# Block products, seven for eight, in the FFN and mixer output projections, with the residual kept tokens x features

## The chip, the cores and the metric

The kernel runs on one core of one Trainium2 chip, in one launch. Its metric is the device time in microseconds of that core, from the start to the end of an execution. The core's engines each run their own instructions in a fixed order and meet through semaphores: TensorE (PE) multiplies matrices, and its weight loads run beside its matmuls; VectorE (DVE), ScalarE (ACT) and GpSimd (POOL) work elementwise; SyncE (SP) issues DMAs, and ACT and POOL can issue them too.

## The reference

A trunk of two layers over 512 tokens of 1024 features in fp32. Each layer is a half-step FFN, a mixer (HGRN2 in layer 0, forgetting attention, called fox, in layer 1) and a second half-step FFN; each of the six sub-layers takes the RMS norm of the residual and adds its result to it. The FFN is the SwiGLU with 2816 hidden features, so its input product is 512 x 1024 by 1024 x 5632, its output product 512 x 2816 by 2816 x 1024.

```python
def rmsnorm(x, g):
    return x * lax.rsqrt(jnp.mean(x * x, axis=-1, keepdims=True) + EPS) * g

def swiglu(h, w_in, w_out):
    gate, up = jnp.split(h @ w_in, 2, axis=-1)
    return (jax.nn.silu(gate) * up) @ w_out

for layer in range(2):
    x = x + 0.5 * swiglu(rmsnorm(x, norm_g[layer, 0]), ffn_w_in[layer, 0], ffn_w_out[layer, 0])
    hn = rmsnorm(x, norm_g[layer, 1])
    x = x + (hgrn2_mixer(hn, ...) if layer == 0 else fox_mixer(hn, ...))   # both end in o @ w_out, 1024 x 1024
    x = x + 0.5 * swiglu(rmsnorm(x, norm_g[layer, 2]), ffn_w_in[layer, 1], ffn_w_out[layer, 1])
```

## The kernel before

*Precision.* Every fp32 operand of the large products is split into two parts of a type that PE takes in one pass: ACT copies it to `h`, rounded, and DVE subtracts `h` from the operand to get `l` (`split_w`, L109: ACT at L113, DVE at L114). A product is then three matmuls into one PSUM bank, `h h`, `h l` and `l h` (`mm3`, L117). Weights come from DRAM in each layer and are split after the load.

*The residual* lies in `xT`, features x tokens: eight tiles of 128 features by 512 tokens. It is made at the start by 32 transposes of x and turned back by 32 at the end (`store`, L629), two tiles of features after each quarter of the last output product. When a tile of `xT` is updated, `norm_tile` (L130) at once makes the next layer's `xh` and `xl` from it, scaled by the norm's gain, and adds its squares up. The root itself is only known when all tiles are done; so the products run on the unnormed rows, and the factor of each token is multiplied onto their results: as a column where tokens are partitions (`norm_col`, L150, its root a power on POOL, L148), as a row spread over the partitions by four transposes where they are columns (`norm_bc`, L169).

*The FFN's input* (`ffn`, L245): 22 tiles of 128 hidden features. For each, the gate and the up product take 8 x 3 matmuls (eight tiles of input features, three parts) with weights of 128x128 and 512 tokens as moving columns (`proj_T`, L179). DVE multiplies both results by the norm's row (L269, L270), ACT does the Silu (L271), DVE the product with `us` (L272), and both split the result. Weights come in loads of 1 MB on SP's queue, two tiles of hidden features at a time.

*The output products* (`out_proj`, L213): four pairs of tiles of 128 output features. Each has 22 (FFN) or 8 (mixer) tiles of input features x 2 x 3 matmuls, again with 512 tokens moving.

*Order.* Pools have numbered buffers: two raw weight tiles, four `wh` and four `wl`, and PSUM banks by tag (three `mm`, two `lv`, two `ms`, one `po`). The order of instructions is that of a scheduler, which follows the program and takes what is ready; on the chip each engine keeps it. The mixers are long chains of their own; of them the change keeps the arithmetic between their input products and their output product.

In the names of tiles below, `f01` is layer 0's second FFN, `g` and `u` gate and up, `o` its output product, `ho` and `xo` the mixers' output products.

## Time and profile before

| What | us |
|---|---|
| median of 3 runs (2080.69 to 2081.03) | 2080.72 |
| the profiled execution | 2079.27 |
| its span, first to last instruction | 2077.5 |
| f00: input product, then output product, end at | 252.3, 372.0 |
| HGRN2, then its output product, end at | 619.2, 672.9 |
| f01: input, output, end at | 913.7, 1033.3 |
| f10: input, output, end at | 1274.1, 1393.8 |
| fox, then its output product, end at | 1642.9, 1708.5 |
| f11: input, output, end at | 1949.3, 2077.5 |

PE is busy in 99% of the span, DVE in 48%, ACT in 35%, POOL in 4%. A stage ends where the first matmul of the next one starts in the timeline of PE (the last one with the span). A busy share says how much of the time some instruction of an engine ran, and since matmuls run over one another, a duration of one is longer than the distance to the next one's start.

### The profile page before, as it was taken

The numbers are of one execution on the slowest core, as the hardware profiler recorded it, in microseconds if no ns is written. First come the engines' busy times: TensorE is split into PE (matmuls) and PEld (weight loads), VectorE is DVE, ScalarE is ACT, GpSimd is POOL, SyncE is SP. The second block draws the span as 40 slices with busy tenths as digits, with TensorE's granted clock in tenths as the row PEclk, the third lists the DMA queues.
The fourth block names the chain that finished last, engine by engine and source line by source line (L and its number), as shares of the span: only waits on it lengthen the run. The fifth ranks groups of instructions, "written<-read, shape, count | busy, mean of one in ns | idle before, by whom it ended". The sixth has DMA issues, their size and how long they took to land.

```text
span 2077.5 us, 23852 instructions
## 1 busy us (share of the span) xinstructions
PE 2059.2 (99%) x9853; PEld 1694.4 (82%) x9853; DVE 1007.1 (48%) x1473; ACT 727.9 (35%) x1083; POOL 77.9 (4%) x90
## 2 busy tenths in 40 slices
PE   8999999999999999999999999999999999999999
PEld 7888888888888888888888888888777778888887
DVE  6444423467566444433344443335566664444332
ACT  5232322333234332322232322227566643232211
POOL 0000000000000000000000000002122100000000
PEclk9999999999999999999999999999999999999999
DMA  5332322221212323322322322333222222232231
GB/s 167 101 102 85 113 92 96 85 76 56 75 60 82 102 81 103 101 97 92 107 91 86 117 82 96 110 98 97 82 68 74 88 72 91 86 117 81 97 116 52
DMA packets 193068, 190.70 MB, mean 92 GB/s; under 512 B 6144, under 2 KB 188848, under 8 KB 192960
## 3 DMA queue, kind: packets, MB, share of 16 engines
q1 hardware_dynamic: 192608, 188.93, 28.1%
q8 instruction: 77, 1.26, 0.2%
q14 instruction: 31, 0.25, 0.0%
q10 hardware_dynamic: 352, 0.25, 0.0%
HBM read 187.04 MB, written 2.13 MB: 91 GB/s over the span
## 4 chain that ended last, share of the span: by engine, by line
PE 94%; ACT 3%; DVE 1%; issue 0%; DMA 0%; SPq 0%
PE f11oy L118 2%; PE f11oy L119 2%; PE f10oy L120 2%; PE f10oy L118 2%; PE f01oy L120 2%; PE f01oy L119 2%; PE f00oy L119 2%; PE f00oy L118 2%; PE f11oy L120 2%; PE f10oy L119 2%; PE f01oy L118 2%; PE f00oy L120 2%; PE lv L358 2%; PE xo L561 1%; PE pT L553 1%; PE xvp L120 1%
## 5 line engine op out<-in xcount | busy, mean ns | idle before, releaser
L538 POOL TENSOR_TENSOR cbc<-cbc,cmask 128x128 f32<-128x128 f32 x64 | 35.3, 552 | 159.7 <-DVE mn L540 106.2
L358 PEld LDWEIGHTS lv<-Q,K 128*128 128x128 f32 x320 | 37.4, 192 | 3.7 <-issue 3.4
L358 PE MATMUL lv<-Q,K 128*128 128x64 f32 x320 | 38.8, 274 | 0.0
L543 ACT ACTIVATE PP<-PP,mn 128x512 f32<-128x512 f32 (+3 forms) x64 | 35.5, 556 | 4.1 <-DVE mn L540 3.4
L120 PE MATMUL xvp<-xvh,xl 128*128 128x256 f32 (+1 forms) x128 | 36.4, 285 | 0.0
L118 PE MATMUL xvp<-xvh,xh 128*128 128x256 f32 (+1 forms) x128 | 36.4, 284 | 0.0
L119 PE MATMUL xvp<-xvl,xh 128*128 128x256 f32 (+1 forms) x128 | 36.4, 284 | 0.0
L134 ACT ACTIVATE xh<-xT,gains 128x512 fp32r<-128x512 f32 x40 | 28.5, 712 | 14.4 <-DVE xT L238 14.4
L558 DVE COPY PP<-pT 128x512 f32<-128x512 f32 (+3 forms) x32 | 15.7, 492 | 35.9 <-PE pT L553 35.9
L553 PEld LDWEIGHTS pT<-ident,PP 128*128 128x128 f32 x160 | 17.0, 140 | 19.6 <-issue 13.2
L540 DVE CUSTOM_DVE_ANT_0 PP<-cbc,sc 128x512 f32<-128x512 f32 (+3 forms) x64 | 30.2, 480 | 3.3 <-PE xo L561 2.6
L135 DVE SCALAR_TENSOR_TENSOR xl<-xT,gains,xh 128x512 fp32r<-128x512 f32 x40 | 29.5, 747 | 4.0 <-ACT xh L134 4.0
L561 PE MATMUL xo<-PP,xV 128*64 128x512 f32 (+3 forms) x128 | 28.2, 458 | 0.0
L536 PE MATMUL sc<-KS,QH 128*128 128x512 f32 (+3 forms) x64 | 22.4, 350 | 5.1 <-DVE mn L540 3.8
L553 PE MATMUL pT<-ident,PP 128*128 128x128 f32 x160 | 24.5, 284 | 2.1 <-DVE PP L545 2.1
L545 DVE TENSOR_SCALAR PP<-PP,mn 128x512 f32<-128x512 f32 (+3 forms) x64 | 26.0, 408 | 1.0
L556 ACT COPY PP<-pT 128x512 f32<-128x512 f32 (+3 forms) x32 | 13.6, 426 | 35.3 <-PE pT L553 34.5
L119 PEld LDWEIGHTS xvp<-xvl,xh 128*128 128x128 f32 x128 | 24.4, 191 | 0.2
L118 PEld LDWEIGHTS xvp<-xvh,xh 128*128 128x128 f32 x128 | 24.4, 191 | 0.2
L120 PEld LDWEIGHTS xvp<-xvh,xl 128*128 128x128 f32 x128 | 24.4, 191 | 0.0
L142 DVE TENSOR_TENSOR acc<-acc,sq 128x512 f32<-128x512 f32 x35 | 24.0, 686 | 0.0
L536 PEld LDWEIGHTS sc<-KS,QH 128*128 128x128 f32 x64 | 12.0, 187 | 14.1 <-DVE mn L540 10.0
(2471 smaller groups left out, 6530.3 us busy)
## 6 DMA issues: line engine op xcount, KB each, us to landing
f01wg<-in_ffn_w_in_dram SPq DMA_DIRECT2D x11, 1024.0 KB, 4.9
f01wu<-in_ffn_w_in_dram SPq DMA_DIRECT2D x11, 1024.0 KB, 4.9
f10wg<-in_ffn_w_in_dram SPq DMA_DIRECT2D x11, 1024.0 KB, 5.1
f10wu<-in_ffn_w_in_dram SPq DMA_DIRECT2D x11, 1024.0 KB, 4.9
f11wg<-in_ffn_w_in_dram SPq DMA_DIRECT2D x11, 1024.0 KB, 5.0
f11wu<-in_ffn_w_in_dram SPq DMA_DIRECT2D x11, 1024.0 KB, 5.0
f00wg<-in_ffn_w_in_dram SPq DMA_DIRECT2D x10, 1024.0 KB, 4.9
f00wu<-in_ffn_w_in_dram SPq DMA_DIRECT2D x10, 1024.0 KB, 4.9
```

The costliest lines, as they stand in the source:

```text
L118: MM(out, lhsT=lh, rhs=rh, start=first, stop=False)
L119: MM(out, lhsT=lh, rhs=rl, start=False, stop=False)
L120: MM(out, lhsT=ll, rhs=rh, start=False, stop=last)
L134: nc.scalar.activation(st["xh"][:, k, :], xT[:, k, :], AF.Copy, scale=g)
L135: nc.vector.scalar_tensor_tensor(st["xl"][:, k, :], xT[:, k, :], g, r32(st["xh"][:, k, :]), op0=ALU.mult, op1=ALU.subtract)
L358: MM(pl[:, c], lhsT=Kc[:, c, :], rhs=Qv[:, c, :, 1, :], start=True, stop=True)
L536: MM(sc[:, :W], lhsT=QH[:, par, ts_], rhs=KS[:, par, :W], start=True, stop=False)
L538: nc.gpsimd.tensor_add(cb[:, ts_], cb[:, ts_], cmask)
L540: nc.vector.tensor_tensor_reduce(row, cb[:, :W].rearrange("p (b s) -> p b s", s=P), sc[:, :W].rearrange("p (b s) -> p b s", s=P), 1.0, 3.0e38,
L543: nc.scalar.activation(row, row, AF.Exp, scale=-1.0, bias=mn[:, t:t + 1], accum_out=sms[par][:, t:t + 1])
L553: nc.tensor.transpose(pT[:, (t - s) * P:(t - s + 1) * P], PPs[par][:, s, t, :], ident)
L561: MM(po[rows, s * P:], lhsT=V[:, s, (pr * 2 + par) * FD:(pr * 2 + par + 1) * FD], rhs=PPs[par][:, s, s:, :].rearrange("p t q -> p (t q)"), ...
```

## The change

*Seven products for eight.* Both matrices of a product are cut into 2 x 2 blocks. Instead of eight block products, sums of blocks are formed on both sides first, and seven products `p1` to `p7` are taken of them; their results are combined by additions. On the activations' side the operands are B11, B21, B22 and the sums T1 to T4; on the weights' side W11, W12, W22 and four sums. The weight sums are made in SBUF by DMAs of POOL's queue that add the loaded block to the tile (`accum_op`): one tile `x` holds W21, then W21+W22, then further blocks, and is split anew each time; one further sum, `s3`, is an addition on POOL. The activation sums are formed on DVE in the FFN's input and on POOL in its output.

*FFN input* (`steps_in`): the two halves of the tokens are the columns of the blocks, so a matmul moves 256 columns. There are 11 items of 256 hidden features from each half (the last with 128 of gate and 128 of up); each has 7 products of 2 x 4 x 3 matmuls, on blocks of 512 input features. ACT and DVE combine the results; the Silu stands on ACT.

*FFN and mixer outputs* (`steps_out`): the result is tokens x features, with weights as the moving operand, 512 columns, and activations as what PE holds. There are 7 products, each over 11 (or 4) tiles of input features x 2 tiles of tokens x 3.

*Residual and norm.* The residual `X` stays tokens x features from the load to the store. After an output product ACT squares it with the sums per token, POOL takes the root, ACT scales the rows by it, PE transposes them (`turn`), and the gain is multiplied on with the copy out of PSUM. The products' inputs are then normed already, so the multiplications by the norm's column or row go.

*Order.* One list of steps, a product or a part of one each, runs through consecutive layers (`Line`): work for a step is written a fixed number of steps ahead (loads 7 to 9, block sums 4 to 8, splits 3). Each tile has a numbered slot of one pool: five `wx` for `x` and `s3`, four `wr`, four `wh` and `wl`, and the eight PSUM banks in turn. The first two items of an FFN run p1, p1, p2, p2 ahead of the rest.

```diff
-    def out_proj(src, nkt, hl, scale, nxt, nm, tail=None, mid=None):
...
-                        if early and kks.start == 2:
-                            mid()
-                        for half in range(2):
-                            hs = slice(half * P, (half + 1) * P)
-                            for kk in kks:
-                                k = k0 + s0 + kk
-                                ah, al = hl[k]
-                                mm3(py[half], h[:, kk, hs], l[:, kk, hs], ah, al, k == 0, k == nkt - 1)
...
+    BUFS = {"ar": 4, "ar3": 2, "wx": 5, "wxs": 1, "wr": 4, "wh": 4, "wl": 4, "bh": 7, "bl": 7,
+            "p1": 3, "V2": 2, "V3": 2, "y": 2, "s": 8}
+    BYTES = {"ar": 8192, "ar3": 6144, "wxs": 2048, "p1": 2048, "V2": 2048, "V3": 2048, "y": 2048, "s": 128}
...
+        def scaled(self, j):
+            self.ys = []
+            for kh in range(2):
+                for t in range(2):
+                    y = at(("V2", "V3")[kh], [T], f"{self.id}y{j}{kh}{t}")
+                    c = 2 * j + t
+                    nc.scalar.activation(y, X[:, c, kh * T:(kh + 1) * T], AF.Copy, scale=rstd[:, c:c + 1])
+                    self.ys.append(y)
...
+            for kp in range(2):
+                pt = psum(f"{self.id}t{j}{kh}{kp}", (2, H))
+                for kk in range(2):
+                    for t in range(2):
+                        k = kp * 2 + kk
+                        nc.tensor.transpose(pt[:, kk, t * P:(t + 1) * P], self.ys[kh * 2 + t][:, k * P:(k + 1) * P], ident)
+                k = kh * 4 + kp * 2
+                if self.blocks:
+                    nc.vector.tensor_mul(self.gx[kh][:, j, kp * 2:kp * 2 + 2, :], pt,
+                                         self.g[:, k:k + 2].unsqueeze(2).to_broadcast([P, 2, H]))
+                    continue
...
+            b11, b12, b21, b22 = self.gx[0][:, 0], self.gx[0][:, 1], self.gx[1][:, 0], self.gx[1][:, 1]
+            nc.vector.tensor_sub(b11, b11, b12)
+            self.block("T1", b11)
+            nc.vector.tensor_sub(b12, b22, b12)
+            self.block("T3", b12)
+            nc.vector.tensor_add(b11, b11, b22)
+            self.block("T2", b11)
+            nc.vector.tensor_sub(b21, b21, b11)
+            self.block("T4", b21)
+            self.block("B22", b22)
...
+            def begin():
+                it["r11"] = load("wr", 0, 0, "r11")
+                it["x"] = load("wx", 0, 1, "x")
+            def sums():
+                it["s3"] = at("wx", [4, 256], n_ + "s3")
+                nc.gpsimd.tensor_add(it["s3"], it["r11"], it["x"])
+                acc(it["x"], 1, 1)
...
+            RAW = {"p1": "r11", "p5": "x", "p2": "r12", "p7": "s3", "p6": "x", "p4": "r22", "p3": "x"}
+            def split_of(p):
+                def what():
+                    it["split"][p] = split(it[RAW[p]], W_HL, [4, 256], f"{n_}{p}")
+                    if p == "p5":
+                        acc(it["x"], 0, 0)
+                    if p == "p6":
+                        acc(it["x"], 1, 0)
+                return what
...
+                    b = {"p2": "p1", "p3": "p5"}.get(p)
+                    if b is None:
+                        it["bank"][p] = psum(f"{n_}{p}", (2, H))
+                    bank = it["bank"][b or p]
+                    h, l = it["split"].pop(p)
+                    bh, bl = norm.B[OPERAND[p]]
+                    for s in range(2):
+                        ss = slice(s * P, (s + 1) * P)
+                        for k in range(4):
+                            mm3(bank[:, s, :], h[:, k, ss], l[:, k, ss], bh[:, k, :], bl[:, k, :],
+                                b is None and s == 0 and k == 0, s == 1 and k == 3, b is not None)
+                return what
...
+                def p6():
+                    it["V2"] = V2 = at("V2", [2, H], n_ + "V2")
+                    it["V3"] = V3 = at("V3", [2, H], n_ + "V3")
+                    nc.vector.tensor_sub(V2, it["p1s"], bank["p6"])
+                    nc.vector.tensor_add(V3, bank["p7"], V2)
+                    result(1, 1, lambda out: nc.vector.scalar_tensor_tensor(out, bank["p5"], -1.0, V3[:, :out.shape[1], :],
+                                                                          op0=ALU.mult, op1=ALU.subtract))
+                def p4():
+                    result(1, 0, lambda out: nc.vector.tensor_sub(out, bank["p4"], it["V3"]))
+                def p3():
+                    result(0, 1, lambda out: nc.vector.tensor_add(out, bank["p5"], it["V2"]))
...
+            steps["p1"].early += [(9, begin), (6, sums)]
+            steps["p2"].early += [(8, load_as("r12", 1, 0))]
+            steps["p4"].early += [(9, load_as("r22", 1, 1))]
+            for p in ORDER:
+                steps[p].early.append((3, split_of(p)))
...
+        items = [item(kind, j) for j in range(NF // 4) for kind in ("g", "u")] + [item("gu", NF // 4)]
+        lead = 2
+        out = [items[i]["p1"] for i in range(lead)] + [items[i]["p2"] for i in range(lead)]
+        for i, it in enumerate(items):
+            out += [it[p] for p in ORDER if i >= lead or p not in ("p1", "p2")]
...
+            st["x"][q] = load(0, 1, q, "wx" if pieces[q][1] == 2 else "wxs", "x")
+            acc(q, 0, 0)
...
+            raw = st["x"][q] if p in ("p7", "p6", "p3") else st["w"].pop((p, q))
+            st["w"]["hl", p, q] = split(raw, W_HL, [pieces[q][1], 512], f"{nm}{p}{q}")
+            if p == "p7":
+                acc(q, 1, 1)
+            if p == "p6":
+                acc(q, 1, 0)
...
+            b11, b12, b21, b22 = quad(0, 0, g), quad(0, 1, g), quad(1, 0, g), quad(1, 1, g)
+            eng = nc.gpsimd if n2 > 4 else nc.vector
+            if name == "T1":
+                eng.tensor_sub(b11, b11, b12)
+            elif name == "T3":
+                eng.tensor_sub(b12, b22, b12)
+            elif name == "T2":
+                eng.tensor_add(b12, b11, b22)
+            else:
+                eng.tensor_sub(b21, b21, b12)
...
+                bh, bl = st["b"][p, k0 // 4]
+                for t in range(2):
+                    ts = slice(t * P, (t + 1) * P)
+                    for kk in range(n):
+                        k = k0 + kk
+                        mm3(st["bank"][p][t], bh[:, k % 4, ts], bl[:, k % 4, ts], h[:, kk, :], l[:, kk, :], k == 0, k == n2 - 1)
...
+                    elif p == "p6":
+                        V2 = at("V2", [T], f"{nm}V2{t}")
+                        V3 = at("V3", [T], f"{nm}V3{t}")
+                        nc.vector.tensor_sub(V2, st["p1s", t], b[t])
+                        nc.vector.tensor_add(V3, st["bank"]["p7"][t], V2)
+                        add(t, 1, V3, -scale)
+                        add(t + 2, 1, V3, -scale)
+                        add(t + 2, 0, V2, scale)
...
+    def turn_second(norm, steps):
+        steps[0].hooks.append(lambda: norm.scaled(1))
+        steps[2].hooks.append(lambda: norm.turn(1, 0))
+        steps[3].hooks.append(lambda: norm.turn(1, 1))
+        steps[3].hooks.append(norm.other_blocks)
```

The first place is POOL's queue in the input product of f10, items `g2` and `u2`. L300 is the addition that makes `s3`; L292 are the DMAs that add a block to the item's `x`, `x2` standing for two in a row. Now:

```order
L292 DMA f10u1x<-in_ffn_w_in_dram 128x4x256
L292 DMA f10g1x<-in_ffn_w_in_dram 128x4x256
L300 TENSOR_TENSOR f10g2s_10322<-f10g2r_10225,f10g2x 128x1024
L292 DMA f10g2x<-in_ffn_w_in_dram 128x4x256
L292 DMA f10u1x<-in_ffn_w_in_dram 128x4x256 x2
L300 TENSOR_TENSOR f10u2s_10552<-f10u2r_10453,f10u2x 128x1024
L292 DMA f10u2x<-in_ffn_w_in_dram 128x4x256
L292 DMA f10g2x<-in_ffn_w_in_dram 128x4x256 x2
L300 TENSOR_TENSOR f10g3s_10781<-f10g3r_10684,f10g3x 128x1024
```

Before, POOL does the following from the norm of f01 on, through f01, f10 and into the fox stage (`small` and `xrr` hold roots, `one` a constant):

```order
L148 TENSOR_TENSOR orc_4355<-orc6v,nhalf 128x4
L148 TENSOR_TENSOR orc_4374<-orc7v,nhalf 128x4
L148 TENSOR_TENSOR small<-rc02v,nhalf 128x4
L148 TENSOR_TENSOR small<-rc10v,nhalf 128x4
L473 MEMSET one_9546 16x512
```

Where POOL had one small operation for a whole layer, each item now has one addition of 128x1024 and three DMAs, and an item's last two DMAs stand behind the addition and first DMA of the item after it.

The second place is DVE's queue in the same stage. L136 is the `l` part of a weight split, L352 to L376 combine results of products into `act`. Now:

```order
L379 TENSOR_TENSOR act_10610<-f10g2p_10557,f10g2V_10672 128x512
L136 TENSOR_TENSOR f10u2p7l<-f10u2s_10552,f10u2p7h 128x1024
L136 TENSOR_TENSOR f10u2p6l<-f10u2x,f10u2p6h 128x1024
L136 TENSOR_TENSOR f10u2p4l<-f10u2r_10616,f10u2p4h 128x1024
L352 TENSOR_TENSOR act_10610<-f10u2p_10749,act_10610 128x512
L136 TENSOR_TENSOR f10u2p3l<-f10u2x,f10u2p3h 128x1024
L136 TENSOR_TENSOR f10g3p1l<-f10g3r_10684,f10g3p1h 128x1024
L370 TENSOR_TENSOR f10u2V_10900<-f10u2p1s,f10u2p_10875 128x512
L371 TENSOR_TENSOR f10u2V_10901<-f10u2p_10846,f10u2V_10900 128x512
L136 TENSOR_TENSOR f10g3p5l<-f10g3x,f10g3p5h 128x1024
L372 SCALAR_TENSOR_TENSOR f10u2y_10904<-f10u2p_10786,f10u2V_10901 128x512
L376 TENSOR_TENSOR f10u2y_10941<-f10u2p_10916,f10u2V_10901 128x512
```

Before, in the same stage, L114 is the weight split, L269, L270 and L272 the norm's row and the SwiGLU, L276 the split of the result:

```order
L269 TENSOR_TENSOR f10gs_7135<-f10g1p,rbc_7065 128x512
L114 TENSOR_TENSOR f10g3l<-f10wg_7145,f10g3h 128x1024
L270 TENSOR_TENSOR f10us_7136<-f10u1p,rbc_7065 128x512
L272 TENSOR_TENSOR f10us_7136<-f10us_7136,f10gs_7135 128x512
L114 TENSOR_TENSOR f10u3l<-f10wu_7147,f10u3h 128x1024
L276 TENSOR_TENSOR f10al_7142<-f10us_7136,f10ah_7141 128x512
L269 TENSOR_TENSOR f10gs_7207<-f10g2p,rbc_7065 128x512
L114 TENSOR_TENSOR f10g4l<-f10wg_7285,f10g4h 128x1024
L270 TENSOR_TENSOR f10us_7208<-f10u2p,rbc_7065 128x512
L272 TENSOR_TENSOR f10us_7208<-f10us_7208,f10gs_7207 128x512
```

Before, one split of 128x1024 stands among three operations per tile; now splits of the next products, of the `x` tile among them, stand in one queue with the combinations of the products before.

## Rows read from the trace of the kernel before

**Rows 1.** The page: span, busy time by engine, the chain that ended last.

```profile
span 2077.5 us, 23852 instructions
PE 2059.2 (99%) x9853; PEld 1694.4 (82%) x9853; DVE 1007.1 (48%) x1473; ACT 727.9 (35%) x1083; POOL 77.9 (4%) x90
...
PE 94%; ACT 3%; DVE 1%; issue 0%; DMA 0%; SPq 0%
```

**Rows 2.** Busy time by stage: FFN f01 in, then out; first the columns.

```profile
core 0: us, PE busy (x) PEld busy (x) DVE busy (x) ACT busy (x) POOL busy (x), PEclk, DMA share, GB/s
...
672.90:913.70 240.80, 240.80 (x1070) 199.50 (x1069) 111.02 (x134) 74.66 (x92) 1.86 (x1) 1.00 0.30 97
913.70:1033.30 119.60, 119.60 (x529) 99.06 (x528) 40.44 (x45) 31.18 (x37) 0.00 (x0) 1.00 0.28 90
```

**Rows 3.** Timeline of PE, 512 columns (start us, us, ...): first and last of 24.

```profile
699.68 0.39 PE L119 MATMUL f01g2p<-xl,f01g2h 128*128 128x512 f32 x1
...
704.89 0.39 PE L118 MATMUL f01u2p<-xh,f01u2h 128*128 128x512 f32 x1
```

**Rows 4.** Timeline of PE, 256 columns: first and last of 93.

```profile
1485.58 0.28 PE L118 MATMUL xvp<-xvh,xh 128*128 128x256 f32 x1
...
1496.62 0.28 PE L120 MATMUL xvp<-xvh,xl 128*128 128x256 f32 x1
```

**Rows 5.** Timeline of PE: eight transposes.

```profile
1457.37 1.09 PE L553 MATMUL pT<-ident,PP 128*128 128x128 f32 x8 [0.36 <-DVE PP L545]
```

**Rows 6.** Timeline of all engines at the start and at the end.

```profile
0.73 0.44 ACTq L64 DMA_DIRECT2D ident<-in_ident_dram  x1
...
1.76 1.28 ACT L158 ACT_TABLE_LOAD   x1 [1.76 <-issue]
...
10.76 0.70 PE L118 MATMUL f00g0p<-xh,first1h 128*128 128x512 f32 x1
...
2071.80 0.39 PE L120 MATMUL f11oy<-f11ah,f11os_20l 128*128 128x512 f32 x1
```

**Rows 7.** Groups of instructions by line and shape, on four engines.

```profile
L114 DVE TENSOR_TENSOR f10os_8l<-f10ow,f10os_8h 128x1024 fp32r<-128x1024 f32 x4 | 4.9, 1226 | 12.9 <-ACT f10os_8h L113 12.9
...
L272 DVE TENSOR_TENSOR f01us<-f01us,f01gs 128x512 f32<-128x512 f32 x22 | 15.2, 692 | 3.6 <-ACT f01gs L271 1.4
...
L113 ACT ACTIVATE f01os_12h<-f01ow 128x1024 fp32r<-128x1024 f32 x4 | 4.2, 1062 | 8.8 <-PE f01oy L119 5.0 <-PE f01u21p L119 3.9
...
L141 ACT ACTIVATE sq<-xT 128x512 f32<-128x512 f32 x35 | 21.6, 616 | 0.0
...
L414 ACT ACTIVATION_READ_ACCUMULATOR osq<-ho 128x1 f32 x32 | 6.6, 207 | 0.0
...
L114 POOL TENSOR_TENSOR first4l<-first,first4h 128x1024 fp32r<-128x1024 f32 x1 | 2.4, 2410 | 12.7 <-ACT first4h L113 12.7
...
L148 POOL TENSOR_TENSOR small<-rc01v,nhalf 128x4 f32<-128x4 f32 x1 | 1.9, 1914 | 352.3 <-DVE rc01v L147 352.3
...
L120 PEld LDWEIGHTS xvp<-xvh,xl 128*128 128x128 f32 x128 | 24.4, 191 | 0.0
```

**Rows 8.** DMA issues: tiles, engine, count, KB each, median us to landing.

```profile
f01wg<-in_ffn_w_in_dram SPq DMA_DIRECT2D x11, 1024.0 KB, 4.9
...
cbc<-cd SPq DMA_DIRECT2D x16, 256.0 KB, 3.4
...
f01ow<-in_ffn_w_out_dram SPq DMA_DIRECT2D x4, 768.0 KB, 4.3
...
first<-in_ffn_w_in_dram SPq DMA_DIRECT2D x4, 512.0 KB, 5.8
```

**Rows 9.** Timeline of DVE and POOL in the fox stage.

```profile
1645.54 1.22 DVE L114 TENSOR_TENSOR xo_s_4l<-xo_w,xo_s_4h 128x1024 fp32r<-128x1024 f32 x1
1645.70 1.38 POOL L538 TENSOR_TENSOR cbc<-cbc,cmask 128x128 f32<-128x128 f32 x1 [17.16 <-DVE mn L540]
```

**Rows 10.** The same POOL line: min/median/max of its instructions.

```profile
L538 POOL TENSOR_TENSOR cbc<-cbc,cmask x64: 452/462/1378, 1442.6 to 1672.3; 128x128 f32<-128x128 f32 x64
```

1178 lines of the change are left out of this document (676 added, 502 removed).

## Prediction

> **What bounds the kernel now.** I read the page's busy shares and its chain first, then a table of busy time by stage, then single matmuls. The page shows TensorE (PE) busy in 99% of the span and 94% of the chain that ended last on PE [rows 1], so only PE's work and the gaps in it count. The table by stage shows the clock at 1.00 (the level of 2.4 GHz) in the two stages of an FFN, VectorE (DVE) at 111 of 241 us and 40 of 120 us, and the DMA engines at 30% for 97 GB/s and 28% for 90 GB/s, which puts their full rate at some 322 GB/s [rows 2]. PE's own "busy" says nothing of its pace, since matmuls overlap: the pace is the distance of starts. Matmuls of 512 columns start every (704.89 - 699.68) / 23 = 0.2265 us [rows 3]. 1056 of them are 239.2 us, the whole of an FFN's first stage, and 528 are 119.6 us, its second: nothing else is on the path there.
>
> The sum below is made against the profiled execution, 2079.3 us, 1.4 us under the median of 2080.7.
>
> **Products removed.** FFN in (`steps_in`): 11 items of 7 products, each 2 x 4 x 3 matmuls, are 1848 matmuls of 256 columns instead of 1056 of 512. 256-column matmuls start every (1496.62 - 1485.58) / 92 = 0.1200 us in the value projection [rows 4], a little over half of 0.2265. So 221.8 us for 239.2: -17.4 for each of four FFNs, -69.6. That is 7% and not 12.5%, as two halves cost 0.2400.
> FFN out (`steps_out`): the moving operand stays at 512 columns, 7 x 2 x 11 x 3 = 462 for 528: -66 x 0.2265 = -14.9, four times -59.8. The two mixer outputs go from 192 to 168 matmuls each: -10.9. Together -140.3 us.
>
> **Transposes.** The five later norms now turn tokens into features, 32 transposes of 128x128 each. Eight of these took 1.09 us, 0.136 each [rows 5]: +21.8. The 24 of `norm_bc` (-3.3) and the 32 before the output (-4.4) go. Net +14.1.
>
> **The start.** Before, the first matmul of f00 stands at 10.76 us, and another 2.2 us are lost to transposes until the stage's 239.2 us end at 252.3. Now ScalarE (ACT) issues seven DMAs at about 0.5 us, loads its table in 1.28 [rows 6], does eight squares at 0.62 and an accumulator read of 0.21 (12 us so far), four scalings, the splits of B11 and B21 at 1.06, four more scalings, and only then, in its order, the split of the first weight [rows 7]: 12 + 2.6 + 3 + 2.6 + 1.1, about 21.5 us. +11, bounds +5 (the order hurts less) and +16.
>
> **FFN starts after another layer** (three). After the last product p3: two updates of X on DVE (0.69 each), squares, the root (two small operations, 1.91 us on GpSimd (POOL)) and four scalings, about 7.6 us; then 16 transposes, four multiplications, T1 and its split. PE has p1, p1, p2, p2 to do, 4 x 2.88 = 11.5 us and 2.2 us of transposes; it waits 0.5 us at the first transposes. Behind them DVE does nine block operations of 1.23 us beside weight splits of 1.23 [rows 7]: 3.7 us per product, where PE takes 2.88, for four products. I take 3.5 us a start: +10.5, bounds 0 and +20. The mixers' starts have two 5.4 us chunks of matmuls over the same chain, less the turn itself: +2 each, +4.
>
> **The end.** Two transposes, copies and a store follow the last matmul at 2071.80 before [rows 6]; now two updates and a store: -1.
>
> **What lies beside PE in FFN in.** An item takes PE 7 x 2.88 = 20.2 us. DVE does seven splits (8.6) and on average seven operations of 0.69 (4.8), 13.4 us; ACT 7 x 1.06 plus three or four of 0.62, about 10 [rows 7]. Both are covered. What may not be is the chain that builds weight sums. One tile x holds W21, is added to s3 on POOL, gets +W22, is split for p5, gets +W11, is split for p6, gets +W12, is split for p3; each addition is a DMA issued by POOL that adds into SBUF. The order ties items together: s3 of the item after next takes x's slot, so its POOL addition waits for p3's split, and it stands in POOL's queue, with its own DMA, ahead of the next item's two (the change's first order rows). From one p3 split to the next the loop is: POOL addition 2.41, up to 1.2 that it waits for DVE (below), one DMA issue c, an accumulating DMA T, split 1.06 + 1.23, T, split 1.06 + 1.23, handovers 0.6. That is 8.8 + c + 2T, and it is free up to 20.2. Late items first use up a lead of 6.6 us (p3's split ends 2.3 steps of 2.88 us before PE needs it), then PE waits; with nine such loops a stage loses 9 x (8.8 + c + 2T - 20.2) - 6.6.
>
> No such DMA is in the trace before. From below: a plain load of 512 KB lies between 256 KB at 3.4 us and 768 KB at 4.3 [rows 8], 3.85. From above: 5.8, the 512 KB loads of the crowded start, plus 1 us of POOL's issue (its small operations are 1 to 1.9) and 1.6 for reading the destination as well (512 KB at 322 GB/s): 8.4. I take 3.85 + 1.6 = 5.4, as the loads at steady state are the nearer row, and c = 1. The loop is then 20.6: 0.4 x 9 is inside the lead, nothing is lost. The Trainium skill ("DMA: Bandwidth & Descriptors", Anatomy of one DMA) gives 2.0 us plus bytes over 436 GB/s for a DMA issued by GpSimd; by that estimate T would be 3.2, and the loop, at 16.2, would be hidden with room; no run here shows it.
>
> **What lies beside PE in FFN out.** PE takes 104.7 us. DVE: 7 x 6.8 for weight splits, 7 x 3.4 for activation splits, 22 updates of 0.69, 5 for the next norm: 92 us. It fits, at 88%. POOL does 12 block sums, 26.7 us, and issues 24 accumulating DMAs. When POOL's two-input addition met a DVE split of two SBUF inputs (1.22 us from 1645.54), it took 1.38 us [rows 9] instead of its line's median of 0.46 [rows 10]: it waited for DVE. In this direction DVE loses nothing, and that is the term: 0. The Trainium skill ("SBUF - State Buffer", Who interferes with whom) says that whichever of the two issues first keeps the port and the other blocks fully; the trace agrees for POOL's wait, and shows no DVE operation behind a POOL one. By that rule DVE would also stand behind POOL's sums, which is the second rival.
>
> Mixers inside: some 60 multiplications by the norm's row go from DVE, and a few copies come to ACT, none of them on PE's path: 0, or up to -10.
>
> **Sum.** 2079.3 - 140.3 + 14.1 + 11 + 10.5 + 4 - 1 = 1977.6, with 1.4 to the median 1979; I predict 1980.
>
> **Rivals.**
> *The accumulate loop sets the pace (slower).* Place: POOL's queue in the four FFN-in stages. It costs the whole gain of 101 us from T = 6.95 on (25 us a stage). With T = 7.2 the loop is 24.2 us, the loss 29.4 a stage, 118 in all: 2098; at the bound of 8.4 it is 26.6, 51 a stage: 2184. For it: rows 8 show 5.8 us for a plain 512 KB in a crowded queue, and an item now moves 3.67 MB in 20.2 us, 182 GB/s, nearly twice the 97 of before [rows 2]. Against: T must be 80% above a plain load.
> *DVE behind POOL's sums in FFN out.* 92 + 26.7 = 118.7 us, 14 over PE's 104.7, four times 56: 2036. For: the port is shared, as rows 9 show. Against: POOL is the one that waits there, and splits run three steps ahead of PE.
> *DMA engines in FFN out.* Nine quadrants of 2.88 MB are 26.0 MB in 104.7 us, 248 of 322 GB/s. If the four accumulated ones cost twice, 37.5 MB need 116.5 us: +11.8, four times 47: 2027. For: no transfer before adds in place. Against: 77% if they cost once.
> *Half the columns don't save half the time.* Were a matmul bound by its weight load, 0.191 us [rows 7], FFN in would take 353 us, 454 more in all. Against: those very matmuls start every 0.120 us [rows 4].
>
> **Chances.** Forecast (1945 to 2005) 0.52; DVE behind POOL 0.14; DMA engines, or a loop a little too long, 0.13; the loop at pace 0.20, of which 0.03 land within 0.2% of before; the last 0.01. A difference of 0.2%, 4 us, is about what can be told from none. So faster 0.79, same 0.03, slower 0.18. The range: below, the lower bounds of start, FFN starts and mixers (-6, -10.5, -4, -10) give 1949, so 1945; above, up to 2100 to hold the milder half of the loop's case. The forecast's own range is 1945 to 2005.
>
> **What would show it.** Starts of 256-column matmuls 0.120 us apart in `f10g2p...`, and 512-column ones 0.2265 in `f10o`; f00's first matmul near 21 us; PE idle of 2 to 5 us at p5 to p6 of the first item; stages FFN in near 225 us and FFN out near 105. If FFN in is 240 or more with ACT and DVE waiting for DMA on x, the first rival holds, and T from the DMA view says so; if FFN out is 115 or more, splits that are longer than 1.23 us mean the port, DMA shares near 1 mean the engines. A first stage over 300 us would mean that the pace of rows 4 does not carry over.

## The result, and the profile after

The changed kernel takes 2405.0 us (median of 4 runs, 2403.8 to 2409.4) against 2080.7: a ratio of 1.156, 95% interval 1.154 to 1.158. The forecast was 1980, its range 1945 to 2100. Its terms add up to 1977.6 us for the profiled execution, and so to a span of 1975.8, as the span before was 1.8 us shorter than its execution. The profiled span is 2403.1: 427 us are missing. This table says where. Bounds are the first matmuls of each product in PE's timeline; the column of the prediction spreads its terms over the stages.

| us | before | predicted | after | after less predicted |
|---|---|---|---|---|
| start, to the first matmul of f00 | 10.8 | 21.8 | 28.7 | +7 |
| four FFN inputs | 963.9 | 909.1 | 1155.7 | +247 |
| four FFN outputs | 487.3 | 428.6 | 560.2 | +132 |
| two mixers with their outputs | 615.6 | 616.3 | 658.6 | +42 |

The output's first product runs among the last matmuls of the input, so some 15 us a stage (5 in the faster kernels below) could stand in the row above.

The page of the changed kernel, beside [rows 1]:

```profile
span 2403.1 us, 31939 instructions
PE 2089.2 (87%) x12773; PEld 1842.7 (77%) x12773; DVE 1497.7 (62%) x1818; ACT 1023.0 (43%) x1475; POOL 657.6 (27%) x443
...
PEclk8899899999999899989998998999999989999899
...
q0 software_dynamic: 104448, 123.75, 32.4%
q1 hardware_dynamic: 189344, 202.44, 27.0%
...
PE 20%; DMA 12%; DVE 7%; ACT 4%; issue 4%; POOL 1%; ACTq 0%; POOLq 0%; DVEq 0%
```

PE is busy for 87% of the span instead of 99%, and it is no longer the chain: its share there fell from 94% to 20%, DMA has 12%. `q0` is POOL's queue: 124 MB of added blocks take 32.4% of the DMA engines' time, 202 MB of plain loads 27.0%, so an added byte costs twice a loaded one. PEclk is no longer 9 throughout. The stages of f01, in and out, beside [rows 2] (same columns; the bound between them is here the input's own last matmul):

```profile
776.55:1083.60 307.05, 253.50 (x1876) 246.28 (x1877) 180.63 (x180) 112.87 (x133) 88.49 (x53) 0.91 0.67 142
1083.60:1206.70 123.10, 111.18 (x468) 88.95 (x467) 92.39 (x88) 62.56 (x78) 53.71 (x31) 0.96 0.77 179
```

PE idles for 54 of 307 us in the input and 12 of 123 in the output, and the granted clock (the column behind the engines) is 0.91 and 0.96. What a lower clock costs is seen on PE's timeline at the start of f00, at rows of the same 256-column matmul, with three windows under it:

```profile
19.89 0.45 PE L194 MATMUL n00t<-ident,n00y 128*128 128x128 f32 x2 [2.49 <-ACT n00y L178]
...
27.48 1.54 PE L194 MATMUL n00t<-ident,n00y 128*128 128x128 f32 x6 [5.38 <-ACT n00y L178]
...
31.18 0.41 PE L145 MATMUL f00g0p<-n00B11h,f00g0p1l 128*128 128x256 f32 x1
...
33.95 0.41 PE L143 MATMUL f00g0p<-n00B11h,f00g0p1h 128*128 128x256 f32 x1
...
34.71 0.28 PE L144 MATMUL f00g0p<-n00B11l,f00g0p1h 128*128 128x256 f32 x1
...
35.65 0.28 PE L145 MATMUL f00u0p<-n00B11h,f00u0p1l 128*128 128x256 f32 x1
```

```profile
17.60:20.90 3.30, 0.84 (x6) 0.61 (x7) 3.30 (x2) 2.73 (x4) 3.30 (x2) 1.00 1.19 310
21.00:28.00 7.00, 1.62 (x9) 1.23 (x8) 3.87 (x7) 1.46 (x4) 2.31 (x3) 0.50 1.31 223
31.00:34.50 3.50, 3.50 (x18) 3.50 (x18) 3.39 (x4) 0.21 (x1) 0.00 (x0) 0.50 0.77 234
```

From 31.18 on, 13 starts lie (33.95 - 31.18) / 13 = 0.213 us apart at a clock of 0.50 (1.2 GHz); then 8 starts lie 0.118 apart, the pace of [rows 4]. The clock had fallen by 21 us, after the wait of 2.49 us that ends at 19.89; the wait of 5.38 us in front of the last transposes (at 27.48) lies inside the slow stretch and did not start it. Where PE waits, the matmuls behind can thus be slower too, and the prediction had no term for that; what it comes to in f01's input is worked out below, at the additions on DVE.

In the input product POOL's queue shows the pace (line L300 is the addition that makes `s3`, one per item; the `L292` rows are additions by DMA):

```profile
905.27 2.40 POOL L300 TENSOR_TENSOR f01g3s<-f01g3r,f01g3x 128x1024 f32<-128x1024 f32 x1 [8.63 <-DVE f01g2p3l L136]
907.97 1.30 POOL L292 DMA_DIRECT2D f01g3x<-in_ffn_w_in_dram  x1 [0.30 <-POOL f01g3s L300]
911.51 1.28 POOL L292 DMA_DIRECT2D f01u2x<-in_ffn_w_in_dram  x1 [2.24 <-DVE f01u2p5l L136]
921.45 1.28 POOL L292 DMA_DIRECT2D f01u2x<-in_ffn_w_in_dram  x1 [8.66 <-DVE f01u2p6l L136]
931.60 3.29 POOL L300 TENSOR_TENSOR f01u3s<-f01u3r,f01u3x 128x1024 f32<-128x1024 f32 x1 [8.87 <-DVE f01u2p3l L136]
```

From one `s3` to the next it is 931.60 - 905.27 = 26.3 us, where PE needs 20.2. The two DMAs issued at 911.51 and 921.45 are the second and third addition of item `u2`: between them, and behind the second, lie 10 us each. The view of the DMA issues (KB each, median us to landing) has their length:

```profile
f01g2x<-in_ffn_w_in_dram POOLq DMA_DIRECT2D x3, 512.0 KB, 7.9
...
f01u3x<-in_ffn_w_in_dram POOLq DMA_DIRECT2D x3, 512.0 KB, 6.3
```

In the output product, DVE's splits (first fence) stand beside POOL's block sums (second fence):

```profile
1097.61 3.41 DVE L136 TENSOR_TENSOR f01op21l<-f01op,f01op21h 128x1024 fp32r<-128x1024 f32 x1
...
1113.15 1.21 DVE L136 TENSOR_TENSOR f01obp61l<-act,f01obp61h 128x1024 fp32r<-128x1024 f32 x1
```

```profile
1096.95 2.98 POOL L452 TENSOR_TENSOR act<-act,act 128x1024 f32<-128x1024 f32 x1
1099.90 3.38 POOL L450 TENSOR_TENSOR act<-act,act 128x1024 f32<-128x1024 f32 x1
```

A split that takes 1.21 us alone takes 3.41 beside them. PE waits there for these splits (`op21`, `op24`) and for those of p5 (`op51`, `op53`), in the view of waits (us in total, times, longest):

```profile
PE f01op L143 <- ACT f01op53h L135: 4.2, 1, 4.2
PE f01op L144 <- DVE f01op24l L136: 2.5, 1, 2.5
PE f01op L143 <- ACT f01op51h L135: 2.0, 1, 2.0
PE f01op L144 <- DVE f01op21l L136: 1.8, 1, 1.8
```

At the start, the first matmul stands at 28.67 instead of the forecast 21.5. On ACT a small exponential of HGRN2's lower bounds, written ahead of the first weight split, waits for its DMA (by way of DVE's L123); and DVE's first split, beside POOL's second `s3`, takes 4.18 us:

```profile
26.60 0.21 ACT L124 ACTIVATE cols<-cols 128x8 f32<-128x8 f32 x1 [5.54 <-DVE cols L123]
```

```profile
18.05 4.18 DVE L136 TENSOR_TENSOR n00B11l<-n00g,n00B11h 128x1024 fp32r<-128x1024 f32 x1
```

### The profile page after: what moved, and what is told of

Its sections match the earlier page's. It is cut to its first block, busy times and chain, and to the rows that moved or that the text cites. A ratio compares the mean times of both kernels' runs of the same rounds, so it can differ in the third digit from the quotient of the medians.

```text
span 2403.1 us, 31939 instructions
## 1 busy us (share of the span) xinstructions
PE 2089.2 (87%) x12773; PEld 1842.7 (77%) x12773; DVE 1497.7 (62%) x1818; ACT 1023.0 (43%) x1475; POOL 657.6 (27%) x443
## 3 DMA queue, kind: packets, MB, share of 16 engines
q0 software_dynamic: 104448, 123.75, 32.4%
## 5 line engine op out<-in xcount | busy, mean ns | idle before, releaser
L345 ACT ACTIVATE act<-act 128x512 f32<-128x512 f32 x60 | 37.0, 628 | 76.2 <-DVE act L372 72.4
L446 POOL TENSOR_TENSOR act<-act 128x1024 f32<-128x1024 f32 (+1 forms) x12 | 40.4, 3366 | 63.2 <-DVE act L355 45.4
L452 POOL TENSOR_TENSOR act<-act,act 128x1024 f32<-128x1024 f32 (+1 forms) x12 | 36.3, 3026 | 0.9
L448 POOL TENSOR_TENSOR act<-act,act 128x1024 f32<-128x1024 f32 (+1 forms) x12 | 36.1, 3010 | 0.6
L450 POOL TENSOR_TENSOR act<-act,act 128x1024 f32<-128x1024 f32 (+1 forms) x12 | 35.8, 2980 | 0.0
L420 POOL DMA_DIRECT2D f10ox<-in_ffn_w_out_dram x18 | 21.8, 1215 | 37.5 <-DVE act L352 11.5
L420 POOL DMA_DIRECT2D f11ox<-in_ffn_w_out_dram x18 | 22.4, 1246 | 33.3 <-DVE f11u4y L376 11.1
L420 POOL DMA_DIRECT2D f00ox<-in_ffn_w_out_dram x18 | 22.3, 1240 | 31.9 <-DVE f00gu5p5l L136 13.0
L420 POOL DMA_DIRECT2D f01ox<-in_ffn_w_out_dram x18 | 22.8, 1268 | 29.4 <-DVE f01gu5p5l L136 11.9
L862 PE MATMUL sc<-KS,QH 128*128 128x512 f32 (+3 forms) x64 | 22.8, 357 | 4.1 <-DVE mn L866 2.5
L687 DVE TENSOR_TENSOR Q<-Q,tot 128x512 f32<-128x512 f32 x24 | 16.6, 692 | 15.3 <-PE lv L677 11.8
## 6 DMA issues: line engine op xcount, KB each, us to landing
f11ox<-in_ffn_w_out_dram POOLq DMA_DIRECT2D x15, 512.0 KB, 10.8
```

The source lines that it names most:

```text
L345: nc.scalar.activation(out, out if ps_ is None else ps_, AF.Silu)
L420: nc.gpsimd.dma_start(st["x"][q], rows(kh, mh, q), accum_op=ALU.add)
L446: eng.tensor_sub(b11, b11, b12)
L448: eng.tensor_sub(b12, b22, b12)
L450: eng.tensor_add(b12, b11, b22)
L452: eng.tensor_sub(b21, b21, b12)
```

## The experiments

Theory A: the chain of two additions by DMA in a row, with a split behind each, sets the pace of the FFN's input (the prediction's first rival). Theory B: the DMA engines' load sets it, or the landing of one addition, whatever the slots. Further ones (C to S) are named where they are tested. Times of one run each unless said; the changed kernel is 2405, the kernel before 2080.

**Own slots for x and s3.**

```diff
-                it["x"] = load("wx", 0, 1, "x")
+                it["x"] = load("wx", 0, 1, "x", idx % 3)
-                it["s3"] = at("wx", [4, 256], n_ + "s3")
+                it["s3"] = at("wx", [4, 256], n_ + "s3", slot=3 + idx % 2)
```

> Edit: in the FFN's input product x takes three slots of its own and s3 two (the five slots were taken in turn), so that s3 of the item after next no longer waits for the split for p3. All work and all DMAs stay. Theory A (the loop split for p3, POOL addition, DMA, split, DMA, split sets the pace, 24 to 26 us an item where PE needs 20.2): the loop is cut, items fall to 20.5 to 22 us, an FFN's input product from 302 us to 230 to 250, its clock share from 0.91 to over 0.97, the whole from 2405 to about 2170 (2120 to 2230). Theory B (it is the DMA engines' load of 0.67, or that one addition's landing of 6 to 8 us is longer than the three steps by which a split leads, whatever the slots): items stay above 24 us, the whole stays above 2350.

Measured 2404.9: nothing, as theory B had it. The link that the prediction named, s3 waiting for x's slot, isn't needed for the pace. ACT's rows in this run show another one:

```profile
917.86 1.06 ACT L135 ACTIVATE f01u2p3h<-f01u2x 128x1024 fp32r<-128x1024 f32 x1 [6.38 <-DMA f01u2x<-in_ffn_w_in_dram]
918.83 1.04 ACT L135 ACTIVATE f01g3p1h<-f01g3r 128x1024 fp32r<-128x1024 f32 x1
919.77 1.04 ACT L135 ACTIVATE f01g3p5h<-f01g3x 128x1024 fp32r<-128x1024 f32 x1
```

The split for p3 waits for the third addition, and the next item's splits for p1 and p5 stand behind it; the next second addition waits for that p5. The period is about the same, 26.0 us:

```profile
892.97 2.41 POOL L300 TENSOR_TENSOR f01g3s<-f01g3r,f01g3x 128x1024 f32<-128x1024 f32 x1 [6.79 <-DMA f01g3r<-in_ffn_w_in_dram]
...
919.02 3.42 POOL L300 TENSOR_TENSOR f01u3s<-f01u3r,f01u3x 128x1024 f32<-128x1024 f32 x1 [6.64 <-DMA f01u3r<-in_ffn_w_in_dram]
```

**The splits in another order.** Two runs, both with the slots of the last one: first the split for p3 one step ahead of its product, then that for p5 four steps ahead as well.

```diff
-                steps[p].early.append((3, split_of(p)))
+                steps[p].early.append((1 if p == "p3" else 3, split_of(p)))
```

> Edit: the own slots of x and s3 of the run before, and the split for p3 one step ahead of its product instead of three, so that on ACT and DVE it stands behind the next item's splits for p1 and p5 and no longer ahead of them. All work and all DMAs stay. With the slots alone the time did not move, and ACT's rows show the split for p3 waiting for the third addition while the next item's splits, ready, stand behind it. Theory A2 (the loop is the two DMAs in a row, and what closes it is the order of the splits on ACT and DVE, not the slot of x): items fall from 25.2 to 20.3 to 22 us, the FFN's input product to 240 to 260, the whole to about 2210 (2170 to 2280). Theory B (the load of the DMA engines, or the landing of one addition, sets the pace whatever the order): over 24 us an item, over 2350.

Measured 2368.5, over theory B's 2350; the items still take some 24 us, and the split for p5 still stood behind p3's.

```diff
+                steps[p].early.append(({"p5": 4, "p3": 1}.get(p, 3), split_of(p)))
```

> Edit: as the run before with own slots and the split for p3 one step ahead, but the split for p5 now four steps ahead instead of three. In that run the next item's split for p5 still stood behind p3's on ACT, both being written at the same step, and the period fell only from 25.2 to 24.3 us. Now it stands ahead of it. All DMAs and all work stay. Theory A2 (what closes the loop is that the next item's split for p5, and with it its second addition, stands behind the split for p3, which waits for the third): items fall to 20.3 to 22 us, the FFN's input product from 295 to 240 to 260, the whole to about 2230 (2180 to 2290). Theory B (the DMA engines' load, or an addition's landing, sets the pace in any order): items stay at 24 us, the whole at 2350 or more.

Measured 2400.4, again a miss of theory A and inside theory B's words: the items now take 26 to 29 us. The split for p5 is ahead, but POOL's queue closes the loop: the addition for s3 waits 19 us for its W11, whose load waits for a slot, and the second and third addition of the items before stand behind it.

```profile
885.97 3.36 POOL L300 TENSOR_TENSOR f01g3s<-f01g3r,f01g3x 128x1024 f32<-128x1024 f32 x1 [19.10 <-DMA f01g3r<-in_ffn_w_in_dram]
889.62 1.30 POOL L292 DMA_DIRECT2D f01g3x<-in_ffn_w_in_dram  x1 [0.30 <-POOL f01g3s L300]
890.42 1.82 POOL L292 DMA_DIRECT2D f01g2x<-in_ffn_w_in_dram  x1
```

So there are loops through slots, ACT's order and POOL's order, and cutting one leaves another of 24 to 29 us. Which of them closes it in the changed kernel is not settled, and these three runs alone speak for theory B; whether its load or the two DMAs in a row are the long part is what the next runs test.

**The same DMAs without the addition.**

```diff
-                    nc.gpsimd.dma_start(w[:, :, i * n:(i + 1) * n], ap, accum_op=ALU.add)
+                    nc.gpsimd.dma_start(w[:, :, i * n:(i + 1) * n], ap)
```

> Edit: the DMAs on POOL's queue in the FFN's input product write the block instead of adding it (the sums of weights are left out, so the products are of other matrices; everything else is in place, the loop and POOL's issues too). It measures what the addition itself costs a DMA. Theory A (reading the destination is what makes these DMAs 6.3 to 7.9 us long): they land in 4 to 5 us, the loop of 26 us falls by 2 x 2.5 to about 21, the whole to about 2200 (2150 to 2260). Theory C (POOL's issue of 1.3 us and its software queue make them long, not the addition): they still take over 6 us, the whole stays within 50 us of 2405.

Measured 2236.9. On the same queue those of f01 land in 4.0 to 5.1 us instead of 6.0 to 7.9, POOL's issue takes 0.75 instead of 1.3, and the period is 20.5 us here (22.8 at the next):

```profile
f01g3x<-in_ffn_w_in_dram POOLq DMA_DIRECT2D x3, 512.0 KB, 5.1
...
f01u3x<-in_ffn_w_in_dram POOLq DMA_DIRECT2D x3, 512.0 KB, 4.3
```

```profile
868.94 3.24 POOL L300 TENSOR_TENSOR f01u3s<-f01u3r,f01u3x 128x1024 f32<-128x1024 f32 x1 [6.52 <-DMA f01u3r<-in_ffn_w_in_dram]
...
889.47 2.41 POOL L300 TENSOR_TENSOR f01g4s<-f01g4r,f01g4x 128x1024 f32<-128x1024 f32 x1 [6.86 <-DVE f01g3p3l L136]
```

Theory C falls: it is not the queue. From 800 to 880 us that queue's share of the DMA engines is 24.2% for 5.82 MB here and 38.5% for 4.72 MB in the changed kernel, twice as much per byte. The lighter load has a part in the landings, as SP's plain loads of f01's items `g2` to `u4` land sooner too (3.9 to 4.7 us for 5.5 to 6.3); but at the same load (0.59 against 0.60 of the engines, 820 to 960 us) the additions that are left in the next run take 5.9 to 7.6 us.

**The second and third addition on DVE.**

```diff
-                    if p == "p5":
-                        acc(it["x"], 0, 0)
-                    if p == "p6":
-                        acc(it["x"], 1, 0)
+                    if p in ("p5", "p6"):
+                        if idx < 2:
+                            acc(it["x"], *((0, 0) if p == "p5" else (1, 0)))
+                        else:
+                            nc.vector.tensor_add(it["x"], it["x"], it["r11" if p == "p5" else "r12"])
```

> Edit: from the third item on, the second and third addition to x are done by DVE from the tiles of W11 and W12 that are in SBUF for p1 and p2 anyway; the two DMAs go (18 of 33 accumulating DMAs of an FFN's input product stay away). Theory A: the loop loses both of its DMAs of 7 us, items fall to 20.5 to 22 us, the input product to 230 to 245, the whole to about 2160 (2110 to 2210); DVE at 16 of 20 us an item does not bind. Rival D (DVE, at 180 us of 302 already, is what the splits wait for): 9 x 2.5 us of more DVE work lengthen the stage to over 310, the whole to over 2430.

Measured 2209.3, -196, at the upper end of what theory A expected. In the same 140 us of f01's input, first the changed kernel, then this one:

```profile
820.00:960.00 140.00, 120.14 (x893) 118.00 (x893) 81.13 (x78) 49.94 (x56) 38.62 (x23) 0.90 0.66 144
```

```profile
820.00:960.00 140.00, 140.00 (x1164) 139.29 (x1164) 108.47 (x114) 61.55 (x68) 29.79 (x16) 1.00 0.59 143
```

PE is busy throughout at a clock of 1.00, with 1164 matmuls for 893. By these rows the waits cost the changed kernel twice: PE idles for 19.9 of the 140 us, and its 893 matmuls take 120.1 / 893 = 0.1345 us each instead of 0.1203, another 12.7 us. DVE's 2.5 us more per item did not bind there.

**The load put back, off the chain.** Both of these runs lighten the DMA engines too, so this one adds two accumulating DMAs per item into s3's tile after its last use.

```diff
+                    if idx >= 2 and p in ("p7", "p3"):
+                        acc(it["s3"], *((0, 0) if p == "p7" else (1, 0)))
```

> Edit: the run with the second and third addition on DVE (2209 us), and beside it two DMAs with an addition per item from its third on, of the same 512 KB blocks as the two that went, into the tile of s3 after its last use, where nobody reads them. The DMA engines and POOL's queue so carry what they carried in the changed kernel, off the chain. Theory A (the length of the chain of two additions in a row sets the pace): items stay at 20.3 us, the whole within 2205 to 2240. Theory B (the load of the DMA engines, some 0.67, sets it): items go back to 24 us or more, the whole above 2340.

Measured 2207.6, as without them. In the same 140 us the DMA engines' share (second column from the end) is higher than it was in the changed kernel, and PE does not wait:

```profile
820.00:960.00 140.00, 139.35 (x1157) 138.43 (x1156) 108.28 (x113) 61.94 (x69) 46.99 (x30) 1.00 0.87 185
```

The load, as theory B had it, falls: the engines carry 0.87 and PE is busy for 139.4 of 140 us. Its other half, that one addition lands late, is a part of the chain and stays. It is the length of the chain.

**Block sums of the output on DVE.**

```diff
-            eng = nc.gpsimd if n2 > 4 else nc.vector
+            eng = nc.vector
```

> Edit: the block sums of the activations in the FFN's output product are formed by DVE instead of POOL (12 a stage). Theory E (POOL's sums and DVE's splits hold up each other: 12 sums of 3.0 to 3.4 us for 2.4, splits beside them of 2.2 to 3.4 us for 1.2): DVE's splits are 1.22 us again, DVE does the sums in 12 x 1.22 = 15 us, and the waits of PE for splits of p2 (some 5 us and their lower clock) go: the output product is 6 to 12 us shorter, the whole 2360 to 2385. Rival F (DVE is full there, 89 of 123 us): the stage is some 10 us longer, the whole about 2440.

Measured 2351.0, -54, a little more than expected; the outputs fall from 560 to 510 us. Splits beside the sums (L446 to L452, now on DVE) take 1.22 us, as the sums do, where POOL took 3:

```profile
1080.23 1.22 DVE L450 TENSOR_TENSOR act<-act,act 128x1024 f32<-128x1024 f32 x1
...
1084.01 1.22 DVE L136 TENSOR_TENSOR f01obp60l<-act,f01obp60h 128x1024 fp32r<-128x1024 f32 x1
```

Theory E holds, and DVE is not full (F falls). The Trainium skill ("SBUF — State Buffer", Who interferes with whom) has DVE and GpSimd lock a shared port against each other; here the trace agrees in both directions, with 1.2 us grown to 3.4 on DVE and 2.4 to 3.4 on POOL.

**p5's operand from the tile that p4 has loaded**, p4 and p5 in turns, beside the last edit.

```diff
+            if p == "p5" and mixed:
+                nc.vector.tensor_add(raw, raw, st["w"].pop(("r22", q)))
...
+            turns[4 * nq:6 * nq] = [(p, q) for q in range(nq) for p in ("p4", "p5")]
```

> Edit, beside the block sums on DVE (2351 us alone): in the output products with the order p4, p5 (the FFNs' and HGRN2's) their pieces alternate, and W12 + W22 for p5 is added by DVE from the tile of W22 that p4 has loaded, so that the six loads with an addition behind them on POOL's queue become six plain loads. Theory G (p5's operand needs a load of 4.8 us, an issue of 1.2 and an addition of 7 to 9 in a row with four tiles, and so comes late: PE waits 5 to 8 us at p5 in each stage, and the clock falls): the waits at p5 go, 4 x 8 us and the clock's part, 2351 to 2300 (2285 to 2320). Rival F (DVE at 93 of 119 us is full): within 15 of 2351.

Measured 2302.5, -48 on the run before: theory G holds, and the outputs are at 463 us. The next norm's first transposes moved behind p5 with this edit, so not all of the 48 us need be p5's operand.

**Together.** The additions on DVE for all eleven items, with the block sums there (and W22's load for the first two items written five steps ahead instead of nine):

```diff
-                        if idx < 2:
-                            acc(it["x"], *((0, 0) if p == "p5" else (1, 0)))
-                        else:
-                            nc.vector.tensor_add(it["x"], it["x"], it["r11" if p == "p5" else "r12"])
+                        nc.vector.tensor_add(it["x"], it["x"], it["r11" if p == "p5" else "r12"])
```

> Edit: second and third addition to x by DVE for all eleven items, the first two as well, and the block sums of the output product on DVE. Both changes alone gave -196 and -54; if they are independent, 2155. Beyond that theory A expects the chain of the first two items of each FFN, which still had its DMAs (PE idle for 8.7 of 40 us there, clock 0.77), to go: 4 x 8 to 13: 2105 to 2125. Rival D (DVE, with nine block operations and four more additions of 1.2 us in the first items, is what they wait for): no gain there, 2150 or more.

Measured 2123.9: 31 us under the two edits' own sum, so the chain of the first two items is worth about that, and theory D falls. With p4 and p5 in turns and s3 on DVE as well:

```diff
-                nc.gpsimd.tensor_add(it["s3"], it["r11"], it["x"])
+                nc.vector.tensor_add(it["s3"], it["r11"], it["x"])
```

> Edit: all of the last two runs together, and s3 on DVE as well, so that POOL does no large operation in an FFN and one DMA with an addition is left per item. If the waits found are the whole of the loss: 2115 - 50 for p5, and some 5 for the start, where DVE's first split took 4.2 us beside POOL's sum: about 2060 (2035 to 2095), under the kernel before. If DVE binds (17.1 us of work an item of 20.2 us, about 100 of 107 in the output product): over 2100.

Measured 2102.5, some 40 more than expected and over 2100, the words for a DVE that binds. The outputs come to 443 us, but the inputs rise from 939 to 970: with s3 on DVE, PE waits at p3 of nearly every item for DVE's combinations (0.6 to 3.0 us each in f01). So s3 went back to POOL, and the lower bounds of HGRN2 behind the first FFN:

```diff
+    lower_bounds()
     act = acts()
     late = hgrn(norms[0, 1], act, parts)
```

> Edit: second and third addition to x on DVE for all items, block sums on DVE, p4 and p5 in turns with W12 + W22 on DVE (s3 stays on POOL), and HGRN2's lower bounds computed behind the first FFN instead of ahead of its first split (at the start ACT waits 5.3 us for their DMA in the run without this). If the parts add up: 2124 - 4 x 11.5 for the output products - 6 for the start: 2072 (2060 to 2085). If DVE, at its limit in the first items of an FFN, gives some of it back: 2085 to 2100.

Measured 2067.4, with the inputs down to 933 us and the first matmul at 21.9 us, where it was 29.5. In its f01, in and out, PE idles for 9 of 236 us and 2 of 112:

```profile
683.00:919.00 236.00, 227.09 (x1842) 225.10 (x1843) 190.13 (x195) 110.94 (x128) 45.14 (x25) 0.98 0.53 134
919.00:1031.00 112.00, 110.23 (x504) 91.01 (x503) 103.54 (x112) 66.48 (x82) 23.44 (x19) 1.00 0.76 181
```

> The kernel of 2067 us in one look, timed against the kernel before: 0.5 to 0.8% faster, interval clear of 1. If the one look was luck: no difference beyond 0.2%.

Twelve runs: median 2072.8 (2065.6 to 2081.1), ratio to the kernel before 0.996, interval 0.995 to 0.998. It is faster than both kernels, than the one before by 0.4%, where the single run had 0.6%. These twelve runs spread over 15.5 us, so a few us between single runs of such a kernel show nothing. One further edit, ACT copying half of the transposed tokens:

```diff
+                if self.blocks and j == 1:
+                    for kk in range(2):
+                        nc.scalar.activation(self.gx[kh][:, j, kp * 2 + kk, :], pt[:, kk, :], AF.Copy, scale=self.g[:, k + kk:k + kk + 1])
+                    continue
```

> Edit: as the one before, and ACT instead of DVE copies the second half of the transposed tokens out of PSUM (eight copies of 0.69 us off DVE, sixteen of some 0.4 us on ACT, at each FFN's start). If DVE is what the first two items of an FFN wait for (their p3 waits 4 to 6 us for DVE's combinations in the run before the last): 4 x 2 to 4 us less, about 2060. If ACT's splits are late instead: the same or slower than without.

Measured 2068.6: no difference that a single run can show; the inputs, at 936 us, are within those of the kernel without it (933 and 942).

**What the rest is.** The kernel of 2067 still lies 90 us over the forecast. Two runs leave DVE's work out at two places.

```diff
+            st["w"]["hl", p, q] = (split_h if n2 == 4 else split)(raw, W_HL, [pieces[q][1], 512], f"{nm}{p}{q}")
```

> Edit, on the kernel of 2067 us (mixers and their output products together 665 us there, 659 in the changed kernel, 616 before): in the two mixers' output products the low parts of the weights are left out on DVE (the high part is used in their place, so that PE does the same matmuls; the results lose precision): 28 splits of 1.22 us off DVE in two stretches of some 50 us. Theory M (DVE, which has 14 + 7 splits and four sums in each of these outputs where it had 8, is what PE waits for, and the clock falls behind the waits): the two mixers with their outputs get 15 to 35 us shorter, 630 to 650. Rival N (the waits are those of additions by DMA for x and p5, or lie in the mixers themselves): within 5 us of 665.

Measured 2062.4, which is inside the spread; but the mixers with their outputs take 650 us, and 662 to 665 in the four traces that have the mixers without this edit. That is at the lower edge of theory M: DVE's splits are some 12 to 15 of the 47 us, the rest stays open.

```diff
+            self.B[name] = split_h(raw, B_HL, [4, H], f"{self.id}{name}")
```

> Edit, on the same kernel: the low parts of the seven operands of the activations in each FFN's input product are left out on DVE (the high part stands in, PE does the same matmuls): 7 splits of 1.22 us less in the first 40 us of each of four stages. Theory S (DVE's nine to eleven block operations beside the weights' splits are what the first two items wait for): the four input products, 933 to 942 us together, get 4 x 4 to 9 us shorter, 905 to 925. Rival (ACT's chain of squares, root and scaling is the limit there): within 5 us.

Measured 2037.9; the four inputs take 906.5 us instead of 933 to 942, near the forecast's 909.1. Theory S holds. The first 40 us of f01's input, in the kernel of 2067 and then here:

```profile
683.00:723.00 40.00, 36.97 (x280) 36.16 (x281) 36.45 (x37) 22.71 (x29) 3.64 (x3) 0.91 0.21 67
```

```profile
676.50:716.50 40.00, 39.87 (x317) 39.43 (x318) 34.43 (x36) 25.29 (x32) 5.38 (x3) 0.96 0.37 99
```

With DVE at 36.5 of 40 us PE misses 3.0 us and runs at 0.91; with DVE at 34.4 it misses 0.1 and runs at 0.96, with 317 matmul rows for 280.

## Why the prediction was wrong

The forecast looked at the right place and priced it wrongly. In the inputs its first rival, given 0.20, is what happened; the outputs lost time by a part of the second, given 0.14, and by a term that was not in the sum (p5).

- *The accumulate loop.* The failed step is "I take 3.85 + 1.6 = 5.4", from which the loop of 8.8 + c + 2T came out at 20.6 and cost nothing. Measured: T is 6.0 to 7.9 us in f01 (7.2 on average) and c 1.3, so 8.8 + 1.3 + 2 x 7.2 = 24.5 against 23 to 28 us (25 on average) on POOL's rows. The formula gives the size, and the term T was too small twice: a plain DMA of that queue takes 4.5 on average rather than 3.85, and with the addition, and the load that it brings, 2.7 us more rather than 1.6. The break-even of 6.95 stood in the text; the choice between bounds of 3.85 and 8.4 by "the nearer row", a plain load at steady state on another queue, was the mistake. By the Trainium skill's estimate ("DMA: Bandwidth & Descriptors", Anatomy of one DMA) T would be 3.2; the runs have 4.0 to 5.1 without the addition. Taking these DMAs off the chain gave -196, for all items some -227.
- *The rival's price* was too small as well: 29 us a stage at T = 7.2, measured some 60 with the start of the stage. It had no term for the clock (12.7 us in 140 of f01's input, beside 19.9 of waits), and none for the first two items of a stage, whose chain has no lead to use up (31 us in all).
- *The link of the loop* was wrong or not needed: taking x's slot out of it changed nothing. That the formula of this loop still comes near the period is in part luck, since the loops that are left are about as long.
- *POOL's sums in the output.* "In this direction DVE loses nothing, and that is the term: 0" failed: -54 us when they go. The row it rested on [rows 9] shows only a POOL operation behind a DVE one; that no row shows the other direction was read as a zero.
- *p5 in the output* was not in the sum at all: its operand is a load and an addition in a row, with four tiles to run ahead in. Taking the addition by DMA away there, with p4 and p5 in turns, gave 48 us.
- *FFN starts.* 3.5 us each was too small by some 7: DVE's splits there are worth 27 to 35 us in all.
- *The mixers.* In the stretches of their outputs PE idles and the clock falls; after, then before:

```profile
700.00:776.55 76.55, 64.93 (x337) 52.16 (x335) 59.63 (x79) 35.47 (x65) 19.59 (x15) 0.91 0.67 152
1860.00:1973.70 113.70, 97.07 (x458) 74.42 (x456) 85.18 (x147) 67.41 (x118) 31.54 (x26) 0.88 0.55 136
```

```profile
619.00:672.87 53.87, 53.16 (x296) 43.73 (x295) 33.14 (x49) 23.59 (x49) 2.02 (x2) 1.00 0.22 71
1635.00:1708.50 73.50, 71.12 (x343) 53.33 (x342) 51.57 (x115) 46.05 (x86) 7.62 (x13) 1.00 0.21 69
```

  The outputs' 24 fewer matmuls each were counted, what their additional splits and sums do to DVE (60 of 77 us, 85 of 114) was not. About 12 to 15 us are shown to be that.
- *The start* was off by 7 us, and that is ACT's wait of 5.5 us for a constant that only HGRN2 needs, with the transposes that it held up: with the constant moved, the first matmul stands at 21.9 (forecast 21.5). DVE's long first split is not on that path; in that run it is as long as before:

```profile
17.94 4.17 DVE L138 TENSOR_TENSOR n00B11l<-n00g,n00B11h 128x1024 fp32r<-128x1024 f32 x1
```

- *Right:* the paces of both matmul shapes once nothing waits (1164 matmuls of 256 columns in 140 us are 0.120 each; in the kernel of 2067 the outputs run at 110 to 112 us for 105 and the transposes), the counts, that DVE's and ACT's total work fits at steady state, and that 7% of an FFN's input, not an eighth, is what half-width matmuls save.

## What to carry to other kernels

On an engine that is busy for 99%, a change that saves it 7% by adding serial steps elsewhere is decided by those steps' latencies, and waits can be paid again in the clock (here 12.7 us on top of 19.9). Before counting a chain of DMAs as hidden, compute at which length it stops being hidden, and if that lies inside the bounds, take the side that costs. Sums of tiles that are in SBUF anyway belong on the engine with room, not on a DMA that fetches them again.
